# The last 256 tokens of a decoder layer's final product and norm, with tokens on partitions

## The chip, the cores and the metric

The kernel runs on one core of one Trainium2 chip. A core has five engines that work side by side and wait for each other by semaphores: TensorE (PE, matrix products into PSUM; its weight loads are shown as PEld), VectorE (DVE), ScalarE (ACT), GpSimd (POOL) and SyncE (SP), which issues the DMA transfers here. The metric is device time in microseconds for one execution; lower is better.

## The reference

One layer of a decoder: 1024 tokens, 1024 features, a windowed attention, an MLP with squared ReLU of hidden width 4096, and a final norm over the features of each token. The change lies in the last lines:

```python
def rms_norm(x, g):
    xf = x.astype(jnp.float32)
    y = xf * lax.rsqrt(jnp.mean(xf * xf, axis=-1, keepdims=True) + RMS_EPS)
    return (y * g.astype(jnp.float32)).astype(x.dtype)
...
def squared_relu_mlp(h, w_up, w_down):
    a = jax.nn.relu(h @ w_up)
    return (a * a) @ w_down
...
        h = h + mix
        h = h + squared_relu_mlp(rms_norm(h, mlp_norm[i]), mlp_w_up[i], mlp_w_down[i])
    return rms_norm(h, final_norm)
```

All data are float32.

## The kernel before

**Layout.** Features lie on the 128 partitions and tokens along the free dimension: the residual `h` is eight tiles `h[m]` of 128 features by 1024 tokens (`hr` in the profile). A norm therefore needs a sum over partitions, which TensorE makes with a column of ones (`colsum`, line 141; `n` in the profile), then the reciprocal root (`rstd`, line 146; `n_st`), then a diagonal matrix of it (`diag`, line 157; `dg`) and a product of ones with that diagonal which spreads one value per token over all partitions (`bcast`, line 161; `n3b`).

**Products.** Each float32 operand is split into a high part rounded to float32r and a low rest, and a product is three matmuls: high by high, high by low, low by high (lines 624 to 630). A matmul loads one operand of 128 by 128 into the array (LDWEIGHTS) and streams the other past it.

**The down projection.** It is made as seven products of half size (Strassen's scheme; lines 1082 to 1099 and `SEQ`), each of 16 groups of 128 hidden features. For every pair of groups, `operands` (line 1088) loads the hidden activations (`hr<-hid`) and one or two blocks of weights (`wd`, `we`), adds or subtracts these on VectorE (`wf`), and splits both operands on ScalarE (high, `dw_h`, `dx_h`) and VectorE (low, `dw_l`, `dx_l`). `evac` (line 1147) adds a finished product to `h`. The first six products run through lines 1162 to 1177 with 512 tokens per matmul.

**The last product** (lines 1179 to 1234) adds to the odd tiles `h[1], h[3], h[5], h[7]`, tokens 512 to 1023, alone; the even tiles are final before it. It keeps all its split operands in SBUF (`keep`) and runs in two halves. The first takes tokens 512 to 767, group by group as the operands come (`gg` counts pairs, 0 to 7; the prediction's "group" is such a pair, 24 matmuls). The second takes tokens 768 to 1023, four output blocks `mp` in turn, each over all 16 groups. In both a matmul loads 128 hidden features by 128 outputs of the weights and streams 256 tokens. Two generators, `fa` (tokens 0 to 511) and `fb` (512 to 767) of `finish` (line 1114), put the final norm of the earlier tokens between the matmuls, one step at each `next`. The norm of the last 256 tokens comes after all matmuls, with `h` times the gain (`hg`) prepared on ScalarE.

**What sets the order.** TensorE runs in the order of the program text (`pe.ordered`, line 167). From line 1065 on the compiler orders VectorE, ScalarE, GpSimd and SyncE itself: by its own estimate of when each is ready, so that a later instruction may stand ahead of an earlier one. Each engine then takes its queue strictly in that order. Temporary tiles come from rings: six of 128 by 1024 (`temp`, line 604: `wf`, `out`, `hg`), four of 128 by 512 (`sqtile`, line 607) and two PSUM tiles `mm` (`mmtile`, line 96).

Of the kernel before, what the change touches and what calls it, by code (L numbers as in the profile page):

```python
# [6 lines left out]
F32 = mybir.dt.float32  # L7
F32R = mybir.dt.float32r
I32 = mybir.dt.int32
AF = mybir.ActivationFunctionType  # L10
ALU = mybir.AluOpType
# [3 lines left out]
P = 128  # L15
T = 1024
DM = 1024
KT = DM // P
# [4 lines left out]
NG = DFF // (2 * P)  # L23
EPS = 1e-6
# [35 lines left out]
            self.steps.pop(0)()  # L60


def trunk(tc, xT, gains, wqkv, wo, wup, wdn, bias_d, sinks_d, ident_d, mask_d, outT):

# [7 lines left out]
    nc = tc.nc  # L74
    v, s, g, pe = (Ordered(tc, e) for e in (nc.vector, nc.scalar, nc.gpsimd, nc.tensor))

    const = tc.alloc_tile_pool(name="const", bufs=1)
# [3 lines left out]
    def atile(dt, name):  # L81
        return big.tile([P, 1024], dt, tag="A", name=name, bufs=16)
# [13 lines left out]
    def mmtile(name):  # L96
        return pmm.tile([P, 512], F32, tag="mm", name=name)

    ident = const.tile([P, P], F32, name="ident")
    ones = const.tile([P, P], F32, name="ones")  # L100
    mask = const.tile([P, P], I32, name="mask")
    gn = const.tile([P, 3, KT], F32, name="gn")
# [8 lines left out]
    def mm(out, lhsT, rhs, start, stop, **kw):  # L111
        pe.matmul(out, lhsT=lhsT, rhs=rhs, start=start, stop=stop, **kw)
        if tiny:
            tiny.pop(0)()

    def tr(out, in_):
        pe.transpose(out, in_, ident)
# [56 lines left out]
    def small(tag, name):  # L174
        return patt.tile([P, 512], F32, tag=tag, name=name)
# [7 lines left out]
    HALVES = (slice(0, 512), slice(512, 1024))  # L183
# [20 lines left out]
    for k in range(KT):  # L204
        xh = atile(F32R, f"xh{k}")
        xl = atile(F32R, f"xl{k}")
        for sl in HALVES if k < 2 else (slice(0, 1024),):
            nc.sync.dma_start(xr[k][:, sl], xT[:, k, sl])
            if k == 0 and sl.start == 0:
# [4 lines left out]
                                   op0=ALU.mult, op1=ALU.subtract)  # L214
# [32 lines left out]
    VV, KH, KL, h = [], [], [], []  # L247
# [240 lines left out]
    for hf in range(2):  # L488
        ps = small(("pv", "pt")[hf], f"n1_{hf}")
# [111 lines left out]
    def two(tile_):  # L601
        return tile_.rearrange("p (a c) -> p a c", a=2)

    def temp(name):
        return mlp.tile([P, 2, 512], F32, tag="t4", name=name, bufs=6)

    def sqtile(name):
        return mlp.tile([P, 512], F32, tag="sq", name=name, bufs=4)
# [47 lines left out]
    def stat_bcast(hf):  # L656
        ps = bank("Y", f"n2b{hf}")
        bcast(4, ps, stat.pop(("dg", hf)))
        return ps
# [230 lines left out]
    def oblock(m, hf):  # L890
        ps = bank(obanks[(hf * KT + m) % 5], f"o1_{m}_{hf}")
        for kk in range(4):
            mm3(ps, wsl(ws[m // 2], (m % 2) * 4 + kk), o_t[4 + kk], HALVES[hf], kk == 0, kk == 3)
        return ps
# [9 lines left out]
    rb = None  # L904
    for m in range(KT):
# [3 lines left out]
        ps = oblock(m, 1)  # L909
        if m == 0:  # L910
            stat_sum(0)
        if m == 1:
            rb = stat_bcast(0)
# [30 lines left out]
    rb = stat_bcast(1)  # L944
# [143 lines left out]
    def operands(n, gg, alloc):  # L1088
        a, b, op = DOWN[n]
        xr_ = two((qtile if n == SEQ[0] else ktile)(F32, f"hr{n}_{gg}"))  # L1090
        nc.sync.dma_start(xr_, hid[n - 1][gg])
        wr = two(rtile(f"wd{n}_{gg}"))
        nc.sync.dma_start(wr, wdn[a, gg])
        if op is not None:
            w2 = two(pptile(F32, f"we{n}_{gg}"))
            nc.sync.dma_start(w2, wdn[b, gg])
            wr_, wr = wr, temp(f"wf{n}_{gg}")
            v.tensor_tensor(wr, wr_, w2, op=op)
        return split2(wr, alloc, f"dw{n}_{gg}"), split2(xr_, alloc, f"dx{n}_{gg}")

    fin = {}

    def sumsq(key, parts, cols, eng):

        for m in parts:
            if key not in fin:
                fin[key] = sqtile(f"ssq3{key}")[:, 0:cols.stop - cols.start]
                s.activation(fin[key], h[m][:, cols], AF.Square)
            else:
                sq = sqtile(f"sq3_{key}_{m}")[:, 0:cols.stop - cols.start]  # L1110
                s.activation(sq, h[m][:, cols], AF.Square)
                eng.tensor_tensor(fin[key], fin[key], sq, op=ALU.add)

    def finish(t0, t1, sums, tags):

        sl, n = slice(t0, t1), t1 - t0
        nb = n // P
        ps_s = bank(tags[0], f"n3_{t0}")
        for i, sq in enumerate(sums):
            colsum(ps_s, sq, nb, i == 0, i == len(sums) - 1)  # L1120
        rn3 = rstd(ps_s, nb, f"n3_{t0}")
        dg = sqtile(f"dg{t0}")
        diag(rn3, 0, nb, dg)
        yield
        ps = bank(tags[1], f"n3b_{t0}")
        bcast(nb, ps, dg)
        if t1 == T:

            rb = ps[:, 0:n].unsqueeze(1)
            for i in range(2):  # L1130
                k, hg = 4 - i, hgs[i]
                v.tensor_tensor(hg[:, 0:k], hg[:, 0:k], rb.to_broadcast([P, k, n]), op=ALU.mult)
                if i:
                    v.scalar_tensor_tensor(hg[:, k], h[7][:, sl], gn[:, 2, 7:8], ps[:, 0:n],
                                           op0=ALU.mult, op1=ALU.mult)
                nc.sync.dma_start(outT[:, 4 * i:4 * i + 4, sl], hg)
            return
        for mp in range(4):
            yield
            out = temp(f"out{t0}_{mp}")  # L1140
            for e in range(2):
                m = 2 * mp + e
                v.scalar_tensor_tensor(out[:, e, 0:n], h[m][:, sl], gn[:, 2, m:m + 1], ps[:, 0:n],
                                       op0=ALU.mult, op1=ALU.mult)
            nc.sync.dma_start(outT[:, 2 * mp:2 * mp + 2, sl], out[:, :, 0:n])

    def evac(n, ps4, c0, c1):

        for mp, ps in enumerate(ps4):
            for mb, hf, sign in INTO[n]:  # L1150
                m = 2 * mp + mb
                dst = h[m][:, hf * 512 + c0:hf * 512 + c1]
                if sign > 0:
                    v.tensor_tensor(dst, ps, dst, op=ALU.add)
                else:
                    v.tensor_tensor(dst, dst, ps, op=ALU.subtract)
# [5 lines left out]
    for k, n in enumerate(SEQ[:-1]):  # L1162
# [8 lines left out]
        if k == 0:  # L1171
            h = []
# [6 lines left out]
    n = SEQ[-1]  # L1179
    keep = []  # L1180
    last_tags = [qtile] * 8 + [atile] * 8 + [wtile] * 6 + [otile] * 6 + [pptile, pptile, ktile, ktile]
    banks = [bank("X", f"d{n}_{i}") for i in range(3)] + [bank("Z", f"d{n}_3")]

    ps_q = [[banks[2 * q + mp % 2][:, (mp // 2) * 256:(mp // 2) * 256 + 256] for mp in range(4)] for q in range(2)]

    def lalloc(dt, name):
        return last_tags.pop(0)(dt, name)

    def mmq(q, g_, mp, first):
        (wh, wl), (xh, xl) = keep[g_]  # L1190
        c, tq = slice(mp * P, mp * P + P), slice(q * 256, q * 256 + 256)
        ps = ps_q[q][mp]
        mm(ps, wh[:, c], xh[:, tq], first, False, skip_group_check=True)
        mm(ps, wh[:, c], xl[:, tq], False, False, skip_group_check=True)
        mm(ps, wl[:, c], xh[:, tq], False, g_ == NG - 1, skip_group_check=True)

    fa = None
    hgs = []
    for gg in range(NG // 2):
        wv_, xv_ = operands(n, gg, lalloc)  # L1200
        for e in range(2):
            keep.append((wv_[e], xv_[e]))
            for mp in range(4):
                mmq(0, 2 * gg + e, mp, 2 * gg + e == 0 and mp < 2)
        if gg < 4:
            sumsq("b", (2 * gg,), HALVES[1], g)
        if gg == 4:
            fa = finish(0, 512, [fin["a"]], ("Y", "Y"))
        if gg >= 4 and gg % 2 == 0:
            next(fa)  # L1210
    evac(n, ps_q[0], 0, 256)
    sumsq("c", (1, 3, 5, 7), slice(512, 768), v)
    fb = finish(512, 768, [fin["b"][:, 0:256], fin["c"]], ("mm", "mm"))
    for mp in range(4):
        for g_ in range(NG):
            mmq(1, g_, mp, g_ == 0 and mp < 2)
            if g_ in (5, 11):
                next(fa, None)
            if mp > 0 and g_ in (3, 13):
                next(fb, None)  # L1220
        dst = h[2 * mp + 1][:, 768:1024]
        v.tensor_tensor(dst, ps_q[1][mp], dst, op=ALU.add)
        if mp < 3:
            sumsq("d", (2 * mp + 1,), slice(768, 1024), v)
            if mp % 2 == 0:
                hgs.append(temp(f"hg{mp}").rearrange("p a c -> p (a c)").rearrange("p (a c) -> p a c", a=4))
            for m in (2 * mp, 2 * mp + 1) if mp < 2 else (4, 5, 6):
                s.activation(hgs[m // 4][:, m % 4], h[m][:, 768:1024], AF.Copy, scale=gn[:, 2, m:m + 1])
        else:
            sq = sqtile("sq3_last")[:, 0:256]  # L1230
            s.activation(sq, dst, AF.Square)
    for f in (fa, fb, finish(768, 1024, [fin["b"][:, 256:512], fin["d"], sq], ("Y", "Y"))):
        for _ in f:
            pass

    pml.release()
    dram.release()
# [40 lines left out]
```

## Time and profile before

| | |
|---|---|
| time, median of 3 runs | 931.25 us (930.19 to 934.24) |
| profiled execution | 930.74 us |
| its span | 929.0 us |
| TensorE busy | 98% of the span |
| VectorE, ScalarE, GpSimd busy | 74%, 48%, 31% |
| last product's first matmul | 868.84 us |
| last VectorE instruction starts | 924.22 us |

The profile is one execution as recorded on the chip. A row of its timeline gives the start in us from the span's beginning, the duration in us, the engine, the line (here nearly always L41, a helper that records every operation), the operation, output<-inputs by the program's names, and the shape; in brackets stands how long the engine was idle before, and what it waited for. A row "x4" merges four instructions. A row of the groups gives the count, the total us and the mean ns of one. Matmuls overlap: the distance between two starts tells their pace, not their duration. A row of the stretches (from:to) lists for each engine the busy us and instructions, then TensorE's granted clock, the busy share of the DMA engines and their GB/s.

### The profile page before, as it was taken

What the parts mean: (1) busy time and instruction counts of PE and PEld (TensorE: products, weight loads), DVE (VectorE), ACT (ScalarE), POOL (GpSimd) and SP (SyncE); (2) the same over time, 40 slices, a digit from 0 to 9 for tenths busy, and PEclk for the clock granted to TensorE, in tenths of its full rate; (3) what the DMA queues carried; (4) which work ended last, traced back from release to release, by engine and by line L of the source; (5) the groups of instructions that cost most, each with busy time, mean ns of one, the idle gap of its engine ahead of it and who ended that gap; (6) DMA issues with size and microseconds to landing.
All of it is one profiled execution on the core that took longest, in us unless ns stands there. A gap on an engine that the chain in (4) does not pass through costs nothing.

```text
span 929.0 us, 12593 instructions
## 1 busy us (share of the span) xinstructions
PE 910.4 (98%) x4508; PEld 766.4 (82%) x4508; DVE 689.6 (74%) x952; ACT 446.9 (48%) x855; POOL 289.7 (31%) x255
## 2 busy tenths in 40 slices
PE   8999999999999999999999999999999999999996
PEld 7788888888878787888888888788888888888995
DVE  7789988999838998866666575556878786568953
ACT  8578878777524374333333433343343333445511
POOL 1026656566265025664454434110000000040200
PEclk9999999999999999999999999999999999999998
DMA  8200100501354016644444454799788998448522
GB/s 312 69 29 29 53 23 13 204 29 47 115 174 165 1 62 232 205 159 155 164 157 137 145 170 172 274 335 408 286 311 298 339 338 314 164 158 272 205 92 90
DMA packets 57438, 160.36 MB, mean 173 GB/s; under 512 B 6432, under 2 KB 10272, under 8 KB 57376
## 3 DMA queue, kind: packets, MB, share of 16 engines
q1 hardware_dynamic: 57376, 159.57, 48.7%
q8 instruction: 35, 0.57, 0.3%
q14 instruction: 27, 0.22, 0.1%
HBM read 121.79 MB, written 37.75 MB: 172 GB/s over the span
## 4 chain that ended last, share of the span: by engine, by line
PE 86%; DVE 7%; ACT 3%; DMA 1%; issue 1%; POOL 1%; SPq 0%; DVEq 0%; ACTq 0%
PE d L41 33%; PE uX L41 16%; PE f L41 12%; PE uY L41 9%; PE uZ L41 4%; PE pv L41 3%; PE S L41 3%; PE o L41 2%; PE pt L41 1%; PE psv L41 1%; PE psk L41 1%; DMA wu0b<-wup 1%; DVE h L41 1%; DVE oa L41 1%; DVE ta L41 1%
## 5 line engine op out<-in xcount | busy, mean ns | idle before, releaser
L41 PE MATMUL d<-dx_h,dw_h 128*128 128x512 f32 (+1 forms) x512 | 186.3, 364 | 0.0
L41 PE MATMUL d<-dx_h,dw_l 128*128 128x512 f32 (+1 forms) x512 | 185.6, 362 | 0.0
L41 PE MATMUL d<-dx_l,dw_h 128*128 128x512 f32 (+1 forms) x512 | 185.6, 362 | 0.0
L41 PEld LDWEIGHTS d<-dx_l,dw_h 128*128 128x128 f32 x512 | 96.6, 189 | 15.2 <-issue 0.2
L41 PEld LDWEIGHTS d<-dx_h,dw_h 128*128 128x128 f32 x512 | 96.6, 189 | 15.2 <-issue 0.2
L41 PEld LDWEIGHTS d<-dx_h,dw_l 128*128 128x128 f32 x512 | 96.6, 189 | 15.1
L41 ACT CAST dw_h<-wf 128x1024 fp32r<-128x1024 f32 x40 | 41.9, 1051 | 100.0 <-PE d L41 79.4
L41 DVE TENSOR_TENSOR dx_l<-hr,dx_h 128x1024 fp32r<-128x1024 f32 x56 | 71.7, 1287 | 13.6 <-ACT dx_h L41 13.6
L41 POOL TENSOR_TENSOR ssq3a<-ssq3a,sq_a 128x512 f32<-128x512 f32 x7 | 11.7, 1665 | 212.0 <-ACT sq_a L41 211.6
L41 ACT CAST dx_h<-hr 128x1024 fp32r<-128x1024 f32 x56 | 58.5, 1049 | 36.5 <-DMA hr<-hid 35.1
L41 DVE TENSOR_TENSOR dw_l<-wf,dw_h 128x1024 fp32r<-128x1024 f32 x40 | 49.6, 1242 | 25.5 <-ACT dw_h L41 25.3
L41 POOL TENSOR_TENSOR t<-t,sm 128x512 f32<-128x512 f32 x32 | 33.3, 1041 | 109.9 <-DVE sm L41 109.9
L41 DVE TENSOR_TENSOR wf<-wd,we 128x1024 f32<-128x1024 f32 x40 | 49.4, 1248 | 19.6 <-DMA we<-wdn 12.4
L41 ACT ACTIVATE t<-t,sm 128x129 f32<-128x129 f32 x128 | 50.5, 396 | 11.1 <-DVE sm L41 10.6
L41 PE MATMUL f<-xh,w_h 128*128 128x512 f32 x128 | 53.3, 416 | 0.0
L41 PE MATMUL f<-xl,w_h 128*128 128x512 f32 x128 | 50.4, 394 | 0.0
L41 PE MATMUL f<-xh,w_l 128*128 128x512 f32 x128 | 50.2, 393 | 0.0
L41 POOL TENSOR_TENSOR ob<-ob,oa 128x512 f32<-128x512 f32 x16 | 23.3, 1454 | 78.8 <-DVE ob L41 75.3
L41 ACT COPY oa<-uX 128x512 f32<-128x512 f32 x32 | 18.8, 586 | 55.7 <-PE uX L41 55.7
L41 PE MATMUL uX<-xu_h,wb 128*128 128x512 f32 x128 | 42.1, 390 | 0.7 <-ACT oa L41 0.7
L41 POOL TENSOR_TENSOR oc<-oc,oa 128x512 f32<-128x512 f32 x16 | 21.7, 1358 | 62.3 <-DVE oc L41 62.3
L41 POOL TENSOR_SCALAR_AFFINE_SELECT cur<-hl 128x1024 fp32r<-128x1024 f32 x32 | 39.4, 1233 | 2.0 <-DVE hl L41 2.0
(367 smaller groups left out, 2399.4 us busy)
## 6 DMA issues: line engine op xcount, KB each, us to landing
wd<-wdn SPq DMA_DIRECT2D x56, 512.0 KB, 5.5
hr<-hid SPq DMA_DIRECT2D x56, 512.0 KB, 4.9
we<-wdn SPq DMA_DIRECT2D x40, 512.0 KB, 7.2
hid<-oa SPq DMA_DIRECT2D x32, 256.0 KB, 2.6
hid<-oc SPq DMA_DIRECT2D x32, 256.0 KB, 2.5
hid<-ob SPq DMA_DIRECT2D x32, 256.0 KB, 2.5
w_r<-wqkv SPq DMA_DIRECT2D x8, 512.0 KB, 4.1
h<-xT SPq DMA_DIRECT2D x8, 512.0 KB, 6.3
```

Source lines behind the costliest of these rows:

```text
L41: ins = method(*args, **kw)
```

## The change

The last 256 tokens become two tails of 128 tokens. In a tail the roles in the matmul are swapped: the activations of 128 tokens are loaded and 512 outputs of the weights are streamed, so that the result lies with tokens on partitions and all 512 features of the odd blocks along the free dimension. What of `h` belongs to these tokens is turned by transposes on TensorE, in four calls of `turn` behind pairs 4 to 7 of the first half: the even blocks are squared and summed (ScalarE) and multiplied by the gain row `grow` (VectorE), the odd blocks copied. `grow`, the gain of all features on every partition (512 KB), is a new input, loaded behind the operands of pair 2. `last` adds the product, sums squares along the free dimension, takes the reciprocal root per partition, scales and stores both halves into a new output `outB`, which the host puts behind the other 768 tokens. The squares of the even blocks (`sumsq("b", ...)`) cover tokens 512 to 767 only, where they covered 512 to 1023; the branch of `finish` for the last tokens, its column sums, diagonal and broadcast are gone. The steps of `fa` and `fb` stand at other groups.

```diff
-    ps_q = [[banks[2 * q + mp % 2][:, (mp // 2) * 256:(mp // 2) * 256 + 256] for mp in range(4)] for q in range(2)]
+    ps_q = [banks[mp % 2][:, (mp // 2) * 256:(mp // 2) * 256 + 256] for mp in range(4)]
...
+    tails = [768, 896]
+    hT, sE, grow = {}, {}, []
+
+    def turn(t0, e):
+
+        if t0 not in hT:
+            hT[t0] = temp(f"hT{t0}")
+            sE[t0] = const.tile([P, 4], F32, name=f"sE{t0}")
+        ps = mmtile(f"tr{t0}_{e}")
+        for mp in range(4):
+            tr(ps[:, mp * P:mp * P + P], h[2 * mp + e][:, t0:t0 + P])
+        if e:
+            s.copy(hT[t0][:, 1], ps)
+        else:
+            sq = sqtile(f"sqT{t0}")
+            s.activation(sq, ps, AF.Square, accum_out=sE[t0][:, 0:1])
+            v.tensor_tensor(hT[t0][:, 0], ps, grow[0][:, 0], op=ALU.mult)
+            v.tensor_scalar(sE[t0][:, 1:2], sE[t0][:, 0:1], 1.0 / DM, EPS, op0=ALU.mult, op1=ALU.add)
+
+    def last(i, t0, ps):
+
+        x, st = hT[t0], sE[t0]
+        tt = const.tile([P, 4], F32, name=f"tt{t0}")
+        var, y0, b_, y = (tt[:, k:k + 1] for k in range(4))
+        v.tensor_tensor(x[:, 1], ps, x[:, 1], op=ALU.add)
+        sq = sqtile(f"sqL{t0}")
+        s.activation(sq, x[:, 1], AF.Square, accum_out=st[:, 2:3])
+        v.tensor_tensor(x[:, 1], x[:, 1], grow[0][:, 1], op=ALU.mult)
+        s.activation(y, st[:, 2:3], AF.Sqrt, bias=st[:, 1:2], scale=1.0 / DM)
+        v.tensor_scalar(var, st[:, 2:3], 1.0 / DM, st[:, 1:2], op0=ALU.mult, op1=ALU.add)
+        v.reciprocal(y0, y)
+        v.tensor_tensor(b_, y0, y0, op=ALU.mult)
+        v.scalar_tensor_tensor(b_, b_, -0.5, var, op0=ALU.mult, op1=ALU.mult)
+        v.scalar_tensor_tensor(st[:, 3:4], b_, 1.5, y0, op0=ALU.add, op1=ALU.mult)
+        s.activation(x[:, 0], x[:, 0], AF.Copy, scale=st[:, 3:4])
+        v.tensor_scalar(x[:, 1], x[:, 1], st[:, 3:4], None, op0=ALU.mult)
+        nc.sync.dma_start(outB[i, :, 1], x[:, 1])
+        nc.sync.dma_start(outB[i, :, 0], x[:, 0])
+
     fa = None
     for gg in range(NG // 2):
         wv_, xv_ = operands(n, gg, lalloc)
+        if gg == 2:
+            grow.append(temp("grow"))
+            nc.sync.dma_start(grow[0], grow_d)
...
         if gg < 4:
-            sumsq("b", (2 * gg,), HALVES[1], g)
+            sumsq("b", (2 * gg,), slice(512, 768), g)
+        else:
+            turn(tails[gg // 2 - 2], gg % 2)
         if gg == 4:
             fa = finish(0, 512, [fin["a"]], ("Y", "Y"))
         if gg >= 4 and gg % 2 == 0:
             next(fa)
-    evac(n, ps_q[0], 0, 256)
+    evac(n, ps_q, 0, 256)
     sumsq("c", (1, 3, 5, 7), slice(512, 768), v)
-    fb = finish(512, 768, [fin["b"][:, 0:256], fin["c"]], ("mm", "mm"))
-    for mp in range(4):
+    fb = finish(512, 768, [fin["b"], fin["c"]], ("mm", "mm"))
+    for i, t0 in enumerate(tails):
+        ps = banks[2 + i]
         for g_ in range(NG):
-            mmq(1, g_, mp, g_ == 0 and mp < 2)
-            if g_ in (5, 11):
+            (wh, wl), (xh, xl) = keep[g_]
+            tq = slice(t0 - 512, t0 - 512 + P)
+            mm(ps, xh[:, tq], wh, g_ == 0, False, skip_group_check=True)
+            mm(ps, xh[:, tq], wl, False, False, skip_group_check=True)
+            mm(ps, xl[:, tq], wh, False, g_ == NG - 1, skip_group_check=True)
+            if g_ in (2, 5, 8, 11):
                 next(fa, None)
-            if mp > 0 and g_ in (3, 13):
+            if i == 0 and g_ in (9, 14) or i and g_ in (0, 3, 6):
                 next(fb, None)
...
-    for f in (fa, fb, finish(768, 1024, [fin["b"][:, 256:512], fin["d"], sq], ("Y", "Y"))):
-        for _ in f:
-            pass
+        if i:
+            for f in (fa, fb):
+                for _ in f:
+                    pass
+        last(i, t0, ps)
```

More of the change, by code (lines that the diff above doesn't have):

```diff
@@ L60, in run, with trunk @@
             self.steps.pop(0)()
-def trunk(tc, xT, gains, wqkv, wo, wup, wdn, bias_d, sinks_d, ident_d, mask_d, outT):
+def trunk(tc, xT, gains, wqkv, wo, wup, wdn, bias_d, sinks_d, ident_d, mask_d, grow_d, outT, outB):
     nc = tc.nc
@@ L1126, in finish @@
         bcast(nb, ps, dg)
[L1127 to L1137, printed above, removed]
         for mp in range(4):
@@ L1182, in trunk, with mmq @@
     banks = [bank("X", f"d{n}_{i}") for i in range(3)] + [bank("Z", f"d{n}_3")]
-    ps_q = [[banks[2 * q + mp % 2][:, (mp // 2) * 256:(mp // 2) * 256 + 256] for mp in range(4)] for q in range(2)]
+    ps_q = [banks[mp % 2][:, (mp // 2) * 256:(mp // 2) * 256 + 256] for mp in range(4)]
     def lalloc(dt, name):
         return last_tags.pop(0)(dt, name)
-    def mmq(q, g_, mp, first):
+    def mmq(g_, mp, first):
         (wh, wl), (xh, xl) = keep[g_]
-        c, tq = slice(mp * P, mp * P + P), slice(q * 256, q * 256 + 256)
-        ps = ps_q[q][mp]
+        c, tq = slice(mp * P, mp * P + P), slice(0, 256)
+        ps = ps_q[mp]
         mm(ps, wh[:, c], xh[:, tq], first, False, skip_group_check=True)
@@ L1195, in mmq @@
         mm(ps, wl[:, c], xh[:, tq], False, g_ == NG - 1, skip_group_check=True)
+    tails = [768, 896]
[32 more added lines that the diff above has]
+        nc.sync.dma_start(outB[i, :, 0], x[:, 0])
     fa = None
-    hgs = []
     for gg in range(NG // 2):
         wv_, xv_ = operands(n, gg, lalloc)
+        if gg == 2:
+            grow.append(temp("grow"))
+            nc.sync.dma_start(grow[0], grow_d)
         for e in range(2):
@@ L1203, in trunk @@
             for mp in range(4):
-                mmq(0, 2 * gg + e, mp, 2 * gg + e == 0 and mp < 2)
+                mmq(2 * gg + e, mp, 2 * gg + e == 0 and mp < 2)
         if gg < 4:
-            sumsq("b", (2 * gg,), HALVES[1], g)
+            sumsq("b", (2 * gg,), slice(512, 768), g)
+        else:
+            turn(tails[gg // 2 - 2], gg % 2)
         if gg == 4:
@@ L1210, in trunk @@
             next(fa)
-    evac(n, ps_q[0], 0, 256)
+    evac(n, ps_q, 0, 256)
     sumsq("c", (1, 3, 5, 7), slice(512, 768), v)
-    fb = finish(512, 768, [fin["b"][:, 0:256], fin["c"]], ("mm", "mm"))
-    for mp in range(4):
+    fb = finish(512, 768, [fin["b"], fin["c"]], ("mm", "mm"))
+    for i, t0 in enumerate(tails):
+        ps = banks[2 + i]
         for g_ in range(NG):
-            mmq(1, g_, mp, g_ == 0 and mp < 2)
-            if g_ in (5, 11):
+            (wh, wl), (xh, xl) = keep[g_]
[4 more added lines that the diff above has]
+            if g_ in (2, 5, 8, 11):
                 next(fa, None)
-            if mp > 0 and g_ in (3, 13):
+            if i == 0 and g_ in (9, 14) or i and g_ in (0, 3, 6):
                 next(fb, None)
[L1221 to L1231, printed above, removed]
-    for f in (fa, fb, finish(768, 1024, [fin["b"][:, 256:512], fin["d"], sq], ("Y", "Y"))):
-        for _ in f:
-            pass
+        if i:
[3 more added lines that the diff above has]
+        last(i, t0, ps)
     pml.release()
@@ L1265 @@
     arrays["bias"] = bias.reshape(KT, 2, P, P).transpose(0, 2, 1, 3)
+    arrays["grow"] = np.broadcast_to(a["final_norm"].reshape(4, 2, P).transpose(1, 0, 2).reshape(1, 2, 512), (P, 2, 512))
     arrays["ident"] = np.eye(P, dtype=np.float32)
@@ L1271 @@
     d = {n: nc.dram_tensor(n, x.shape, mybir.dt.from_np(x.dtype), kind="ExternalInput").ap() for n, x in arrays.items()}
-    out = nc.dram_tensor("outT", (P, KT, T), F32, kind="ExternalOutput").ap()
+    out = nc.dram_tensor("outT", (P, KT, 768), F32, kind="ExternalOutput").ap()
+    out_b = nc.dram_tensor("outB", (2, P, 2, 512), F32, kind="ExternalOutput").ap()
     with tile.TileContext(nc) as tc:
         trunk(tc, d["xT"], d["gains"], d["wqkv"], d["wo"], d["wup"], d["wdn"], d["bias"], d["sinks"],
-              d["ident"], d["mask"], out)
+              d["ident"], d["mask"], d["grow"], out, out_b)
     r = _run(nc, [arrays], core_ids=[0])
-    return np.ascontiguousarray(r.results[0]["outT"].transpose(2, 1, 0).reshape(1, T, DM))
+    first = r.results[0]["outT"].transpose(2, 1, 0).reshape(768, DM)
+    rest = r.results[0]["outB"].reshape(2, P, 2, 4, P).transpose(0, 1, 3, 2, 4).reshape(256, DM)
+    return np.ascontiguousarray(np.concatenate([first, rest]).reshape(1, T, DM))
```

## The prediction

> **What bounds the kernel now.** I read first the page's busy times, then the last stage engine by engine in the timeline.
>
> ```profile
> span 929.0 us, 12593 instructions
> PE 910.4 (98%) x4508; PEld 766.4 (82%) x4508; DVE 689.6 (74%) x952; ACT 446.9 (48%) x855; POOL 289.7 (31%) x255
> ```
>
> TensorE is busy nearly all the span, so time can go in two ways only: fewer microseconds of TensorE's own queue, or a shorter tail in which TensorE has finished and the rest of the chip works on the last outputs. The tail is read from three extracts of the timeline: the last rows of TensorE, of VectorE and of ScalarE.
>
> ```profile
> 917.84 0.28 PE L41 MATMUL d<-dx_h,dw_l 128*128 128x256 f32 x1
> 917.96 0.50 PE L41 MATMUL n<-ones,ssq3b 128*128 128x1 f32 x4
> 918.32 0.58 PE L41 MATMUL n<-ones,ssq3d 128*128 128x1 f32 x4
> 919.14 0.61 PE L41 MATMUL n<-ones,sq_last 128*128 128x1 f32 x4 [0.24 <-ACT sq_last L41]
> 921.42 0.76 PE L41 MATMUL n3b<-dg,ones 128*128 128x256 f32 x2 [1.67 <-DVE dg L41]
> ```
>
> ```profile
> 918.16 0.42 DVE L41 TENSOR_TENSOR hr<-d,hr 128x256 f32<-128x256 f32 x1 [4.37 <-PE d L41]
> 920.08 0.16 DVE L41 TENSOR_SCALAR n_st<-n 128x2 f32<-128x2 f32 x1 [1.50 <-ACT n_st L41]
> ...
> 920.94 0.42 DVE L41 TENSOR_TENSOR dg<-ident,n_st 128x256 f32<-128x256 f32 x1
> 922.22 2.09 DVE L41 TENSOR_TENSOR hg<-hg,n3b 128x1024 f32<-128x1024 f32 x2 [0.85 <-PE n3b L41]
> 924.22 0.48 DVE L41 SCALAR_TENSOR_TENSOR hg<-hr,gn,n3b 128x256 f32<-128x256 f32 x1
> ```
>
> ```profile
> 918.68 0.42 ACT L41 ACTIVATE sq_last<-hr 128x256 f32<-128x256 f32 x1 [4.94 <-DVE hr L41]
> 919.79 0.26 ACT L41 ACTIVATE n_st<-n,eps 128x2 f32<-128x2 f32 x1 [0.70 <-PE n L41]
> ```
>
> The last product matmul ends at 917.84 + 0.28 = 918.12, and the span ends at 929.0: a tail of 10.88 us in which nothing is hidden. It is a chain from engine to engine: residual add, square, column sums, the reciprocal root, the diagonal, the broadcast, the scaling, the stores. VectorE ends at 924.22 + 0.48 = 924.70; the last 4.30 us are the store and the closing of the program.
>
> **The second half of the last product.** Before, it is 192 matmuls of 256 token columns; after, 96 of 512 output columns, with the activations as the loaded operand. Both shapes stand side by side where the product before last ends and the last begins:
>
> ```profile
> 863.63 0.39 PE L41 MATMUL d<-dx_l,dw_h 128*128 128x512 f32 x1
> ...
> 868.62 0.39 PE L41 MATMUL d<-dx_h,dw_l 128*128 128x512 f32 x1
> 868.84 0.28 PE L41 MATMUL d<-dx_h,dw_h 128*128 128x256 f32 x1
> ...
> 883.12 0.28 PE L41 MATMUL d<-dx_h,dw_l 128*128 128x256 f32 x1
> ```
>
> The wide ones start every (868.62 - 863.63) / 22 = 0.2268 us, the narrow ones every (883.12 - 868.84) / 119 = 0.1200 us. From the first start to the last end the half took 191 x 0.1200 + 0.28 = 23.20 us and will take 95 x 0.2268 + 0.39 = 21.94: **-1.26 us**. Its bounds are 0 (the swapped operand costs what the wide shape wins) and -1.3. The column sums and the broadcast of tokens 512 to 767 stay between the matmuls in both. The Trainium skill (TensorE: Matmul & The Clock Gate, Back-to-back issue gap) gives N / 2.4 + 2.5 ns for an isolated matmul, 109 and 216 ns here, so that halving the count would win only 0.2 us; this trace has 120 and 227 ns, and by the page's figures the sum below would be -2.1 us.
>
> **The transposes.** Four groups of four go into TensorE's queue behind groups 4 to 7 of the first half. The attention stage has the same operation between the same wide matmuls:
>
> ```profile
> 152.57 0.60 PE L41 MATMUL pt<-ident,t 128*128 128x128 f32 x4
> 152.93 0.48 PE L41 MATMUL f<-xh,w_h 128*128 128x512 f32 x1
> 153.24 0.39 PE L41 MATMUL f<-xl,w_h 128*128 128x512 f32 x1
> ```
>
> A group takes 0.36 us from its start to the next matmul, and that matmul is longer than the one behind it. From the group to the second matmul are 0.67 us, where one spacing would be 0.23: 0.44 us a group, 1.76 for four. The groups behind 4 and 6 stand directly before the column sums and the broadcast of tokens 0 to 511, whose return to the product is paid anyway, so I take **+1.7 us**; the bounds are 4 x 0.36 = 1.4 and 4 x 0.60 = 2.4.
>
> ```profile
> L41 PE MATMUL pt<-ident,t x128: 270/272/331, 60.0 to 238.0; 128*128 128x128 f32 x128
> ```
>
> This is the transpose alone, 0.272 us of duration; paid one after another sixteen would be 4.4 us, which the group of four in 0.36 us speaks against. The Trainium skill (the same page, Part 4: PE-mode transpose) gives about 275 ns for one; counted singly that is 4.4 us and a sum of -0.5 us, and the duration agrees here but the spacing does not.
>
> The groups also need a free PSUM tile, and their readers on VectorE and ScalarE must have run before the group two places on may start. These readers, and VectorE's multiplication by the gain row, are queued among the operand splits:
>
> ```profile
> 876.96 3.44 DVE L41 TENSOR_TENSOR wf<-wd,we 128x1024 f32<-128x1024 f32 x2
> 880.33 1.21 DVE L41 TENSOR_TENSOR dx_l<-hr,dx_h 128x1024 fp32r<-128x1024 f32 x1
> 881.47 1.21 DVE L41 TENSOR_TENSOR dw_l<-wf,dw_h 128x1024 fp32r<-128x1024 f32 x1
> 882.60 1.21 DVE L41 TENSOR_TENSOR dx_l<-hr,dx_h 128x1024 fp32r<-128x1024 f32 x1
> 883.74 1.21 DVE L41 TENSOR_TENSOR dw_l<-wf,dw_h 128x1024 fp32r<-128x1024 f32 x1
> 884.87 0.15 DVE L41 TENSOR_SCALAR n_st<-n 128x4 f32<-128x4 f32 x1
> ```
>
> By lines and places the last four splits are those of groups 6 and 7, and they end at 883.74 + 1.21 = 884.95. TensorE wants group 7 at 868.84 + 168 x 0.12 = 889.0 at the earliest: 4 us of cover. Against it stand VectorE's new multiplication (0.68 us, by a row below) with a tiny instruction, and the load of the gain row, 512 KB, which SyncE issues behind the loads of group 2 and ahead of those of groups 3 to 7:
>
> ```profile
> 860.00:870.00 10.00, 10.00 (x50) 8.47 (x49) 8.77 (x8) 4.96 (x5) 0.00 (x0) 1.00 1.02 383
> ```
>
> The DMA engines are full there at 383 GB/s, so those loads come 512 KB / 383 = 1.4 us later. 1.4 + 0.8 = 2.2 of 4 us: I cost the load and VectorE's work at nothing. Without that cover TensorE would pay the excess, up to 2.2 us. GpSimd's squares of the even blocks halve their width, which nobody waits for. The first 128 tokens' norm runs beside the 48 matmuls (10.9 us) of the second 128.
>
> **The tail.** What is left behind the last matmul, with the nearest row for each step:
>
> ```profile
> L41 DVE TENSOR_TENSOR hr<-d,hr 128x512 f32<-128x512 f32 x36 | 22.6, 681 | 0.0
> ```
>
> ```profile
> L41 ACT ACTIVATE sq_a<-hr 128x512 f32<-128x512 f32 x7 | 4.2, 626 | 3.3 <-DVE hr L41 2.3 <-POOL ssq3a L41 1.0
> ```
>
> ```profile
> 100.05 0.19 ACT L41 ACTIVATION_READ_ACCUMULATOR t<-t,sm 128x1 f32 x1
> 100.14 0.57 ACT L41 COPY t<-S 128x512 f32<-128x512 f32 x1
> ```
>
> ```profile
> L41 DVE TENSOR_TENSOR x<-ta,x 128x512 f32<-128x512 f32 x4 | 2.7, 684 | 0.0
> ```
>
> ```profile
> L41 ACT ACTIVATE xh<-xr,gn 128x512 fp32r<-128x512 f32 x4 | 2.8, 715 | 2.7 <-DMA gn<-gains 1.6 <-DMA xr<-xT 1.1
> ```
>
> Counted from the last matmul's end: the residual add starts at 0.04 (918.16 - 918.12) and ends at 0.72. The square starts 0.10 later, as 918.68 did behind 918.58, takes 0.63, and its row sum is read out by one more instruction (0.19, of which some 0.1 comes on top): 1.55. VectorE meanwhile multiplies by the gain row, which may start when the square has read its input, 0.68 us until about 2.15; the square root (0.26) lies under that. From the variance to the finished root were 920.94 - 920.08 = 0.86 us before, and it is the same five instructions: 2.96. ScalarE then scales the even blocks (0.07 to start, 0.715) until 3.75, while VectorE scales the odd ones in at most 0.68. Column sums (0.61), diagonal (0.42), broadcast (0.76) and the scaling of 2.09 + 0.48 us are gone. For the stores:
>
> ```profile
> DMA to landing us min/median/max: 3.0/3.1/3.2
> ```
>
> ```profile
> outT<-out SPq DMA_DIRECT2D x4, 256.0 KB, 2.1
> ```
>
> The first line is that of the two 512 KB stores that end the kernel, the second that of the 256 KB stores of tokens 512 to 767. Of the 4.30 us behind VectorE's end 3.1 were landing and 1.20 issue and closing. Now the last store is one of two of 256 KB, less than half a microsecond apart: 2.3 us, nearer the second row. The tail is 3.75 + 1.20 + 2.3 = 7.25 instead of 10.88: **-3.6 us**. Bounds: with 2.1 of landing and the gain multiplication behind the root's steps in VectorE's order, 6.8; with 3.1 of landing and the two stores' issue in each other's way (0.4), 8.4. So -4.1 to -2.4.
>
> **The sum** is -1.26 + 1.7 - 3.6 = -3.2 us, between -4.0 (all low ends) and 0 (all high ends). The profiled execution took 930.74 us, 0.5 below the median of the runs, 931.25 (930.19 to 934.24). It becomes 927.5, the median **928.0 us**.
>
> **The rivals.** *Slower: the gain multiplications stand too early in VectorE's queue.* VectorE takes its instructions in the order that the compiler gave them. If the multiplication behind group 4's transposes stands ahead of the row at 876.96, VectorE waits for TensorE's group 4 (883.24 with 0.4 of transposes), and the 5.6 us from that row to 882.60 come after 884.5: group 6 is ready at 890.1, where TensorE wants it at about 887.9 (883.24, a group of 2.88, two groups of transposes and the column sums): 2.2 us. The same ahead of group 7's two splits costs 2.3 more. That is +1.3 us in all, **932.5 us**; it decides from 3.2 us of stall on. Against it speaks the row at 884.87: an instruction of VectorE written at that place, and waiting for the column sums behind group 4, stands behind the last split. For it: the order may change with the program. *The stores set the end:* both 256 KB transfers land as late as the 512 KB ones and the tail is 8.4 us: -2.0 us, **929.2**. For it: they run together. *The transposes run one by one:* 4.4 us instead of 1.7, -0.5 us, **930.7**; the change then does almost nothing. The group rows speak against it. *A faster case:* the tail falls under 6 us, for which no row speaks, or every low end holds and the runs scatter down: 926.5.
>
> **How the numbers follow.** The forecast has 0.70, the store-bound tail 0.12, the late splits 0.08, the single transposes 0.04, the faster case 0.06. 0.5% (4.7 us) is about what a measurement of this kernel can tell from no change; the lines are 926.6 and 935.9. The forecast and all rivals but the last lie between them; with the scatter of the runs at the lower line I give faster 0.12, and slower 0.04 for stalls beyond the one priced: same 0.84. The range runs from 926.0 (the low ends and 1 us of scatter) to 931.3 (the high ends), which leaves out most of the late splits.
>
> **What would show it.** Right: wide rows every 0.227 us in the second half, four groups of transposes of 0.4 us, no idle time on TensorE in the first half, about 3.0 us from the last matmul to the root, stores landing in 2.1 to 2.5. Wrong: TensorE waiting for a split or for the reader of a transposed tile, a tail above 8.4 us, or narrow and wide halves of equal length.

## The result, and the profile after

The changed kernel takes 940.07 us (median of 4 runs, 939.54 to 941.81); the kernel before, on the same chip, 930.72 us. The ratio is 1.0102 [1.0086, 1.0118]: slower by 9.4 us, where 928.0 with a range of 926.0 to 931.3 was forecast. The forecast is wrong, in sign too.

The head of the page, span and busy times:

```profile
span 938.7 us, 12416 instructions
PE 914.8 (97%) x4414; PEld 766.1 (82%) x4414; DVE 688.1 (73%) x957; ACT 447.6 (48%) x857; POOL 290.6 (31%) x255
```

The busy share of TensorE barely moves (98 to 97%) and the span is 9.7 us longer. TensorE runs 94 matmuls fewer and is busy for 4.4 us more. So a part of the loss is waiting, and another part is matmuls that take longer. The waits of TensorE (us in total, times, longest) have two lines that the list of the kernel before does not have:

```profile
PE d L41 <- ACT dw_h L41: 6.1, 2, 3.2
PE d L41 <- DVE dw_l L41: 1.1, 2, 0.6
```

Twice TensorE stands still in the last product until the split weights come, 7.2 us in all. Its timeline shows where, and what follows:

```profile
882.46 0.28 PE L41 MATMUL d<-dx_h,dw_l 128*128 128x256 f32 x1
882.58 0.60 PE L41 MATMUL tr<-ident,hr 128*128 128x128 f32 x4
883.02 0.95 PE L41 MATMUL n<-ones,ssq3a 128*128 128x1 f32 x8
887.14 0.57 PE L41 MATMUL d<-dx_h,dw_h 128*128 128x256 f32 x1 [3.18 <-ACT dw_h L41]
887.51 0.41 PE L41 MATMUL d<-dx_l,dw_h 128*128 128x256 f32 x1
888.48 0.58 PE L41 MATMUL d<-dx_h,dw_l 128*128 128x256 f32 x1 [0.55 <-DVE dw_l L41]
888.86 0.41 PE L41 MATMUL d<-dx_h,dw_h 128*128 128x256 f32 x1
...
893.13 0.41 PE L41 MATMUL d<-dx_h,dw_l 128*128 128x256 f32 x1
...
901.35 0.58 PE L41 MATMUL d<-dx_h,dw_h 128*128 128x256 f32 x1 [2.91 <-ACT dw_h L41]
```

The first stall is at pair 5, directly behind the transposes and column sums of pair 4; the second, at 901.35, at pair 7, behind the transposes and broadcast of pair 6. After each, the narrow matmuls start every (893.13 - 888.86) / 20 = 0.213 us instead of 0.12. The stretches of 5 us give the clock that goes with it (busy us and count of PE, PEld, DVE, ACT, POOL; granted clock; DMA share; GB/s):

```profile
885.00:890.00 5.00, 2.31 (x9) 2.01 (x10) 5.00 (x8) 3.04 (x3) 0.00 (x0) 0.72 0.00 2
890.00:895.00 5.00, 5.00 (x29) 5.00 (x29) 1.37 (x2) 0.59 (x1) 0.00 (x0) 0.60 0.02 3
895.00:900.00 5.00, 3.44 (x24) 2.61 (x23) 1.66 (x3) 0.69 (x2) 0.00 (x0) 1.00 0.00 0
900.00:905.00 5.00, 3.07 (x12) 2.78 (x13) 5.00 (x8) 1.04 (x1) 0.00 (x0) 0.58 0.29 109
```

Each row is a mean over 5 us. In slices of 0.5 us the granted clock is 0.50 for some 6.8 us at each stall, from 887.2 to 894.0 and from 900.8 to 907.7, and 1.00 before and after. Those slow matmuls count as busy, which is why the busy share hides them.

Why do the weights come late? VectorE's timeline between the same times:

```profile
872.32 1.21 DVE L41 TENSOR_TENSOR dx_l<-hr,dx_h 128x1024 fp32r<-128x1024 f32 x1
884.00 0.69 DVE L41 TENSOR_TENSOR hT<-tr,grow 128x512 f32<-128x512 f32 x1 [10.46 <-ACT sqT L41]
...
884.82 1.19 DVE L41 TENSOR_TENSOR wf<-wd,we 128x1024 f32<-128x1024 f32 x1
...
886.00 1.22 DVE L41 TENSOR_TENSOR wf<-wd,we 128x1024 f32<-128x1024 f32 x1
...
887.21 1.22 DVE L41 TENSOR_TENSOR dw_l<-wf,dw_h 128x1024 fp32r<-128x1024 f32 x1
...
898.34 0.69 DVE L41 TENSOR_TENSOR hT<-tr,grow 128x512 f32<-128x512 f32 x1 [6.97 <-ACT sqT L41]
...
899.01 1.21 DVE L41 TENSOR_TENSOR wf<-wd,we 128x1024 f32<-128x1024 f32 x1
```

VectorE idles for 10.46 us ahead of the gain multiplication of the first tail (`hT<-tr,grow`), which waits for transposes that TensorE reaches only at 882.58. Behind it stand the weight sums `wf` of pairs 5 and 6, and behind the second tail's multiplication that of pair 7. Their operands have been in SBUF for long: from 875 to 885 the DMA engines move nothing. SyncE issues the stage's last load at

```profile
866.23 0.42 SPq L1096 DMA_DIRECT2D we<-wdn  x1
```

In the kernel before, the sum for pair 5 ran well ahead of the matmuls that need it, the last two followed at 876.96, and no split was late:

```profile
869.04 1.22 DVE L41 TENSOR_TENSOR wf<-wd,we 128x1024 f32<-128x1024 f32 x1
```

(ScalarE's high part `dw_h` needs `wf`, so TensorE's wait is put down to ScalarE; it is VectorE's order that is late.)

### The profile page after: what moved, and what is told of

Same layout as the page of the kernel before. It is cut to its first block, busy times and chain, and to the rows that moved or that the text cites. A ratio compares the mean times of both kernels' runs of the same rounds, so it can differ in the third digit from the quotient of the medians.

```text
span 938.7 us, 12416 instructions
## 1 busy us (share of the span) xinstructions
PE 914.8 (97%) x4414; PEld 766.1 (82%) x4414; DVE 688.1 (73%) x957; ACT 447.6 (48%) x857; POOL 290.6 (31%) x255
## 4 chain that ended last, share of the span: by engine, by line
PE 85%; DVE 7%; ACT 3%; issue 1%; DMA 1%; POOL 1%; SPq 0%; DVEq 0%; ACTq 0%
PE d L41 33%; PE uX L41 16%; PE f L41 12%; PE uY L41 8%; PE uZ L41 4%; PE pv L41 3%; PE S L41 3%; PE o L41 2%; PE pt L41 1%; PE psv L41 1%; PE psk L41 1%; DVE h L41 1%; DMA wv_r<-wqkv 1%; DMA wu0b<-wup 1%; DVE oa L41 1%
## 5 line engine op out<-in xcount | busy, mean ns | idle before, releaser
L41 PE MATMUL d<-dx_h,dw_h 128*128 128x512 f32 (+1 forms) x448 | 170.0, 379 | 6.1 <-ACT dw_h L41 6.1
L41 PE MATMUL d<-dx_h,dw_l 128*128 128x512 f32 (+1 forms) x448 | 169.9, 379 | 1.1 <-DVE dw_l L41 1.1
L41 PE MATMUL d<-dx_l,dw_h 128*128 128x512 f32 (+1 forms) x448 | 169.6, 379 | 0.0
L41 PEld LDWEIGHTS d<-dx_h,dw_h 128*128 128x128 f32 x448 | 86.5, 193 | 21.8 <-ACT dw_h L41 7.0
L41 PEld LDWEIGHTS d<-dx_h,dw_l 128*128 128x128 f32 x448 | 86.5, 193 | 16.8 <-DVE dw_l L41 1.7
L41 PEld LDWEIGHTS d<-dx_l,dw_h 128*128 128x128 f32 x448 | 86.6, 193 | 15.1
L41 ACT ACTIVATE t<-t,sm 128x129 f32<-128x129 f32 x128 | 50.5, 397 | 10.9 <-DVE sm L41 10.4
```

What stands on the lines that cost most here:

```text
L41: ins = method(*args, **kw)
```

## The experiments

**Theories.** All explain a gain multiplication ahead of the weight sums, or deny that it matters.
- *Ring:* temporaries of one ring (`temp`, six tiles) are handed out in the order of the program text. `hT768` is first written behind pair 4's transposes and stands in the text ahead of the sums of pairs 5 and 6, `hT896` ahead of that of pair 7. A sum cannot be placed ahead of the first write of an earlier tile of its ring.
- *Queue:* the compiler puts a VectorE instruction that waits for TensorE there, whatever tile it writes.
- *Shortage:* `hT768`, `hT896` and `grow` hold three of six tiles, so that a sum waits for a free one.
- For the slow matmuls: *clock*, a granted clock that falls while TensorE is idle; against it *piecemeal*, operands that trickle in.

Each ratio is to the kernel before on the same chip: 930.39 us for claim_both_early, claim_first_early and the two probes, 929.85 for keep_clock, turn_late, claim_both_again and claim_and_fuse, 930.04 for keep_clock_short and changed_again.

**claim_both_early**: the changed kernel, with both `hT` tiles claimed and first written, by a tiny memset on GpSimd, at pair 2. All else stays.

```diff
+    def claim(t0):
+        hT[t0] = temp(f"hT{t0}")
+        sE[t0] = const.tile([P, 4], F32, name=f"sE{t0}")
+        g.memset(hT[t0][:, 0, 0:1], 0.0)
...
             nc.sync.dma_start(grow[0], grow_d)
+            for t0 in tails:
+                claim(t0)
```

> The changed kernel, with one addition: behind the load of the gain row (pair 2) both hT tiles are taken from the ring of temporaries and one column of each is set to zero by GpSimd, so that they have their place before the weight sums wf of pairs 3 to 7 ask for theirs. Nothing else moves. Ring theory (temporaries are handed out in the order of the text, so wf of pairs 5 and 6 wait for hT768, which waits for TensorE's transposes, and wf of pair 7 for hT896): no stall of TensorE above 0.5 us in the first half, no half clock, and the 3.2 us of the forecast, 927.5 us against 930.7 before (926.5 to 928.5). Queue theory (the gain multiplication goes first on VectorE because it stands ahead in the text, whatever tile it writes): unchanged, 940. Shortage theory (three of six temporaries are held to the end, and three are too few for the weight sums): unchanged or worse, 940 or more.

Measured: 926.39 us (926.17 to 927.92), ratio 0.9954 [0.9942, 0.9967], as the ring theory has it and 0.1 us below its range. Its VectorE:

```profile
872.85 2.89 DVE L41 TENSOR_TENSOR wf<-wd,we 128x1024 f32<-128x1024 f32 x2
...
879.07 1.21 DVE L41 TENSOR_TENSOR dw_l<-wf,dw_h 128x1024 fp32r<-128x1024 f32 x1
883.30 0.69 DVE L41 TENSOR_TENSOR hT<-tr,grow 128x512 f32<-128x512 f32 x1 [3.02 <-ACT sqT L41]
```

All sums and splits are done by 880.28, ahead of the multiplication, and TensorE's waits no longer name `d`. The multiplication still waits for TensorE, harmlessly. The tiles are held longer than in the changed kernel, so *shortage* falls; the multiplications themselves are unchanged, which speaks against *queue*.

**claim_first_early**: the same for the first tail alone.

```diff
+            for t0 in tails[:1]:
+                claim(t0)
```

> As the run with both tiles taken early, but only hT768; hT896 is taken by its own first writer as in the changed kernel. The changed kernel loses about 12.5 us against the forecast (9.3 measured and 3.2 not won). Ring theory: the first of the two stalls goes, the second stays, about half of the loss comes back: 934 us (932.5 to 935.5), with one idle stretch of TensorE at pair 7. Queue theory: 940. Shortage theory: 940.

Measured: 934.38 us (933.25 to 935.34), ratio 1.0037 [1.0024, 1.0049]: between the two. The stall at pair 5 is gone, that at pair 7 stays, with its slow matmuls; from its waits, its chain and its stretches:

```profile
PE d L41 <- ACT dw_h L41: 2.9, 1, 2.9
```

```profile
895.03 5.06 PE d L41 x22
```

```profile
895.00:900.00 5.00, 4.97 (x23) 4.97 (x24) 3.03 (x5) 0.00 (x0) 0.00 (x0) 0.50 0.79 297
```

Each tile holds back the sums that follow it in the text, and no others.

**probe_in_ring** and **probe_own_tile**: the kernel *before*, with two tiny instructions behind pairs 4 and 6: one matmul of ones, and a copy of one column of its result to a tile that nobody reads. The tile comes from the ring in the first and stands alone in the second.

```diff
+            ps = mmtile(f"probe_ps{gg}")
+            mm(ps[:, 0:P], ones, ones, True, True)
+            pr = temp(f"probe{gg}")            # in probe_in_ring
+            pr = const.tile([P, 2, 2], F32, name=f"probe{gg}")   # in probe_own_tile
+            v.tensor_copy(pr[:, 0, 0:1], ps[:, 0:1])
             next(fa)
```

> The kernel before, with two small additions: behind the matmuls of pairs 4 and 6 of the first half one matmul of ones into a PSUM tile, and a VectorE copy of one column of it into a temporary of the same ring as wf. Nothing reads the copy. No transposes, no gain row, no new tail. Ring theory: two stalls as in the changed kernel, at pairs 5 and 7, some 12 us with the slower clock: 943 us (940 to 945). Queue theory: the same 943. Shortage theory (the temporaries are given back at once): 931.

> The kernel before with the same two matmuls and two VectorE copies, but the copies go into small tiles of their own and not into the ring. Ring theory: no stall, 931.3 us (the matmuls cost some 0.3 each). Queue theory: 943, as with the ring's tiles. Shortage theory: 931.

Measured: 940.09 us (938.57 to 941.34), ratio 1.0098 [1.0082, 1.0113], with the tile in the ring; 930.89 (929.85 to 932.97), 1.0004 [0.9994, 1.0013], with a tile of its own. VectorE with the ring's tile, and then with its own:

```profile
882.29 0.16 DVE L41 COPY probe<-probe_ps 128x1 f32<-128x1 f32 x1 [8.10 <-PE probe_ps L41]
882.37 1.23 DVE L41 TENSOR_TENSOR wf<-wd,we 128x1024 f32<-128x1024 f32 x1
```

```profile
875.54 3.44 DVE L41 TENSOR_TENSOR wf<-wd,we 128x1024 f32<-128x1024 f32 x2
882.31 1.21 DVE L41 TENSOR_TENSOR dw_l<-wf,dw_h 128x1024 fp32r<-128x1024 f32 x1
884.27 0.16 DVE L41 COPY probe<-probe_ps 128x1 f32<-128x1 f32 x1 [0.75 <-PE probe_ps L41]
```

Two copies of 0.16 us cost the old kernel 9.7 us when they claim a tile of the ring, and nothing measurable when they do not. Where the tile comes from decides whether the sums run ahead; *queue* falls. A claim in the ring brings about such a loss with no transposes, no gain row and no wide matmuls in the kernel. The 940.09 us are less than the 943 expected, and 9.7 us less than the 13.4 worked out for the changed kernel below, since TensorE's waits are shorter, 5.2 us in all instead of 7.2:

```profile
PE d L41 <- ACT dw_h L41: 3.3, 2, 1.7
PE d L41 <- DVE dw_l L41: 1.9, 2, 1.1
```

The clock falls here too, to 0.50 in slices of 0.5 us, for some 3.4 us each time instead of 6.8, though no single wait is above 1.7 us. (The compiler's rule itself is not shown, only the order that it gives; and no run separates asking for a tile from first writing it, as both were moved together.)

**keep_clock**: the changed kernel, with 28 matmuls of ones into a bank that the first half does not use, behind each `next(fa)` at pairs 4 and 6, to fill the stalls.

```diff
+            for _ in range(NWARM):
+                mm(banks[2][:, 0:P], ones, ones, True, True)
```

> The changed kernel with 28 matmuls of ones (128x128, some 0.11 us each) behind the column sums of pair 4 and behind the broadcast of pair 6, where TensorE stands idle for 3 to 5 us. Their result is overwritten. Clock theory (behind each stall 22 matmuls take 5.06 us instead of 2.64 because the granted clock fell while TensorE was idle): the idle time is filled, the clock stays, and 2 x 2.4 = 4.8 us come back: 935.5 us against 940.1 (934 to 937), with the narrow matmuls at 0.12 us behind the stalls. Piecemeal theory (they are slow because their operands come one by one): 940.

Measured: 938.92 us (938.7 to 940.59), ratio 1.0097 [1.0083, 1.0111]; the expected time is missed. Its TensorE shows why:

```profile
882.40 0.95 PE L42 MATMUL n<-ones,ssq3a 128*128 128x1 f32 x8
883.22 6.50 PE L42 MATMUL d<-ones 128*128 128x128 f32 x56
889.47 0.36 PE L42 MATMUL d<-dx_h,dw_h 128*128 128x256 f32 x1
```

The fill was too long: it runs for 889.47 - 883.22 = 6.25 us, where the stall that it was to fill lasted 3.18. A matmul of ones stands in the profile as two records of 0.11 us (x56 for 28), and I had priced it as one. Counted from the column sums, the product resumes 889.47 - 882.40 = 7.07 us later, where the changed kernel takes 4.12 (887.14 - 883.02). The granted clock stays at 1.00 from 880 to 910, but what this won was lost in length, so the run decides nothing by its time.

**keep_clock_short**: the same with 18 matmuls.

> As the run with 28 matmuls of ones behind pairs 4 and 6, with 18 of them. 28 took 6.25 us each time (two passes of 0.11 us a matmul) and ended 2.3 us behind the moment at which the changed kernel's first operand was ready; 18 take 4.0 us and end before the stall does. Clock theory: granted clock 1.00 throughout, the narrow matmuls at 0.12 us, the stalls themselves untouched: 4.8 us less than the changed kernel on the same chip (4 to 5.5), 935.3 us. Piecemeal theory: no less.

Measured: 935.81 us (935.12 to 937.88), ratio 1.0059 [1.0042, 1.0076]. The stretches and two rows of the chain:

```profile
885.00:890.00 5.00, 5.00 (x48) 5.00 (x46) 3.93 (x9) 2.67 (x5) 0.00 (x0) 1.00 0.02 5
890.00:895.00 5.00, 4.85 (x41) 4.64 (x40) 3.45 (x5) 1.91 (x3) 0.00 (x0) 1.00 0.00 0
```

```profile
890.55 2.90 PE d L42 x22
...
902.35 2.90 PE d L42 x22
```

The clock stays at 1.00 and the 22 matmuls behind each stall take 2.90 us where the changed kernel's take 5.06. The splits come as late as before: the first matmul that needs a low part starts 890.55 - 885.09 = 5.46 us behind the start of the column sums, as in the changed kernel (888.48 - 883.02 = 5.46). Beside **changed_again**, the changed kernel on the same chip

> The changed kernel once more, on the same chip as the run with 18 matmuls of ones: 1.010 of before (1.0086 to 1.0118).

which took 940.94 us (939.68 to 941.73), ratio 1.0115 [1.01, 1.013], filling the stalls wins 5.1 us: *clock* holds, *piecemeal* falls.

**turn_late**: the changed kernel, with the four calls of `turn` moved behind the loop over the pairs, so that every sum stands in the text ahead of `hT`.

```diff
-        else:
-            turn(tails[gg // 2 - 2], gg % 2)
...
+    for t0 in tails:
+        for e in range(2):
+            turn(t0, e)
     evac(n, ps_q, 0, 256)
```

> The changed kernel with the four calls of turn moved behind the last pair of the first half, ahead of the residual add of tokens 512 to 767. hT768 and hT896 then ask for their temporaries after all weight sums, without being taken early. Ring theory: as with both tiles taken early, 926.5 (925.5 to 928), with perhaps 1 us lost where the third call waits for a PSUM tile. Queue theory: the multiplications now stand behind all splits in the text, the same. It separates nothing between these two; it tells whether early claiming is needed, or only another place in the text.

Measured: 928.02 us (927.32 to 928.29), ratio 0.9976 [0.9966, 0.9986]. The late splits are gone in this way too, so another place in the text is enough; between *ring* and *queue* this decides nothing, since both have it so. The time lies at the upper end of the range expected (925.5 to 928). The four groups now stand together, and the second pair waits for the readers of the first (a wait of its list):

```profile
PE tr L41 <- ACT hT L41: 0.9, 1, 0.9
```

**claim_both_again** is claim_both_early once more.

> The run with both hT tiles taken early once more, on the same chip as the next one: 0.9954 of before, as measured (0.994 to 0.997).

Measured: 927.05 us (926.39 to 930.14), ratio 0.9965 [0.9952, 0.9979], beside turn_late's 928.02. On both chips it beats the kernel before.

**claim_and_fuse**: claim_both_early, with the gain multiplication and the scaling of the odd blocks as one instruction behind the root, and their store issued by ScalarE instead of SyncE.

```diff
-        v.tensor_tensor(x[:, 1], x[:, 1], grow[0][:, 1], op=ALU.mult)
...
-        v.tensor_scalar(x[:, 1], x[:, 1], st[:, 3:4], None, op0=ALU.mult)
-        nc.sync.dma_start(outB[i, :, 1], x[:, 1])
+        v.scalar_tensor_tensor(x[:, 1], x[:, 1], st[:, 3:4], grow[0][:, 1], op0=ALU.mult, op1=ALU.mult)
+        nc.scalar.dma_start(outB[i, :, 1], x[:, 1])
```

> Both hT tiles taken early; in last the multiplication of the odd blocks by the gain row and the scaling by the root become one instruction of VectorE behind the root, and the odd blocks are stored from ScalarE's queue, so that the two stores don't wait for each other's issue. By the tail of the run with both taken early: the root's steps start 0.6 us sooner, the last store is issued 0.4 us sooner behind the scaling: 0.7 to 1.0 us less, 925.5 (0.9945 of before). If the stores' landing sets the end and not their issue, 0.6.

Measured: 926.23 us (925.93 to 927.77), ratio 0.9961 [0.9948, 0.9973]. The median is 0.8 us below claim_both_again's, the size expected, but the intervals overlap and the 925.5 us expected is missed, so no gain is shown. In the tail, where it was to come from, the profiles show next to none. The last store is issued 3.39 us behind the last matmul's end instead of 3.95, but the two stores now start at one time and land later; first claim_both_early's landing, then this kernel's:

```profile
DMA to landing us min/median/max: 2.0/2.3/2.5
```

```profile
DMA to landing us min/median/max: 2.5/2.7/2.8
```

So the 0.56 us are given back to the transfers; from the last matmul to the span's end it is 7.15 us instead of 7.19 in claim_both_early.

## Why the prediction was wrong

I compare from the last product's first matmul (868.84 before, 868.18 after, 867.49 in claim_both_early) to the span's end, since the stretch ahead of it varies by a few us from one execution to the next. That stage takes 60.16 us before, 70.52 after and 57.11 in claim_both_early. Without the late splits the change brings -3.05 us, where -3.2 was forecast; with them it costs 13.4 us more.

**The terms that held.** claim_both_early shows them undisturbed, in the chain:

```profile
882.05 0.44 PE tr L41 x4
882.49 0.79 PE n L41 x8
...
886.25 0.44 PE tr L41 x4
...
889.57 0.44 PE tr L41 x4
890.00 0.86 PE n3b L41 x2
...
893.73 0.44 PE tr L41 x4
894.16 6.83 PE d L41 x30
...
901.78 3.58 PE d L41 x15
...
905.78 11.62 PE d L41 x51
917.41 0.02 issue
```

- *Second half:* 6.83 + 3.58 + 11.62 = 22.03 us of wide matmuls (forecast 21.94). The kernel before has, in its chain, 10.07, 3.70 and 12.24 us for 216 narrow ones, of which 24 belong to pair 7: 26.01 - 24 x 0.12 = 23.13. That is -1.10 for the forecast -1.26. The swapped operand costs nothing.
- *Transposes:* four groups of 0.44 us are 1.76, forecast 1.7. Counted singly by their duration they would have been 4.4; the pace of a group decides.
- *Tail:* 924.6 - 917.41 = 7.19 us, forecast 7.25; 10.88 before. So -3.7 for -3.6.

**The step that failed** is "I cost the load and VectorE's work at nothing", and behind it the price and the chance of the rival that had the gain multiplications too early in VectorE's queue. The load was free. The order was not, for three reasons.

First, the evidence. Against that rival I set one row: "an instruction of VectorE written at that place, and waiting for the column sums behind group 4, stands behind the last split." But that row writes `n_st`, which is not of the ring of `wf`, and `hT` is. probe_own_tile and probe_in_ring are those two cases side by side, 930.89 and 940.09. An instruction's place was read off one that claimed something else. That the new tile comes from `temp` stood in the diff, and that `wf` does too in the kernel's description.

Second, what is held back. I let the multiplication delay the splits of groups 6 and 7 only, by 2.2 and 2.3 us. It held back the sums, and the first of them, for pair 5, stood at 869.04 before, ahead of the row at 876.96 from which I counted; TensorE wants that pair right behind pair 4. So nothing hides the chain from the transposes to the operands: transposes, square, multiplication, sum, high part, low part. Against claim_both_early TensorE's first matmul behind the inserts comes 3.3 and 3.1 us later (887.14 - 883.02 = 4.12 where its chain has 0.79; 901.35 - 897.42 = 3.93 where it has 0.86), and the wait for the low part costs 1.1 us more each time (888.48 - 887.14 = 1.34 where two spacings are 0.24): 8.6 us.

Third, the clock, which I had not in the sum at all. The 22 matmuls behind each stall take 5.06 us instead of 22 x 0.12 = 2.64: 4.8 us for both. At clock 1.00, in keep_clock_short, they take 2.90, so 2 x (5.06 - 2.90) = 4.3 us of this are the clock's own and the rest stays at full clock; the time fell there by 5.1, in medians whose runs scatter by some 2 us. The Trainium skill (TensorE: Matmul & The Clock Gate, Part 1: The HAM clock gate) has the clock at half after an idle window of about 3.4 us; the trace agrees in the half and has it earlier. The clock falls some 3.2 us after the first wait begins and some 2.4 after the second, and in probe_in_ring waits of 1.69 and 1.07 us with two matmuls between them were enough. A single wait of 1.62 us in the attention stage of the kernel before leaves it at 1.00. The runs do not show where between these the limit lies.

8.6 + 4.8 = 13.4 us, as the stages differ; -3.05 + 13.4 = +10.4 for the stage. The stretch ahead of it was 0.7 us shorter in the changed kernel's profile, so the spans differ by 9.7, and the medians by 9.4. "It decides from 3.2 us of stall on" was right, and so was the rival's direction; it had 8 chances in 100 and a third of its price.

The signs that the forecast gave named the fault ("TensorE waiting for a split") and the parts that held (pace 0.227, groups of 0.4, stores in 2.1 to 2.5).

## What to carry to other kernels

Look where each new tile comes from. As the compiler ordered this kernel, the first write to a tile of a shared ring also fixes the place of all later tiles of that ring, so a tile whose first writer waits for a slow engine needs a claim early in the text, a ring of its own, or a place behind the tiles that others wait for.

When the place of an instruction in a queue is inferred from another instruction, that one must write to the same pool of tiles. And a wait of TensorE of some 3 us, or two close together of 1.7 and 1.1, is to be priced well above its length, since the matmuls behind it run at half the clock: 7.2 us of waits in the list cost 13.4 here.

The version to keep is the change with both tiles claimed early: 0.9954 [0.9942, 0.9967] and 0.9965 [0.9952, 0.9979] of the kernel before, 4.0 and 2.8 us, about what was forecast.

## What was not expected of the hardware

- A fill of TensorE with 18 matmuls of ones, whose result nobody uses, made the changed kernel 5.1 us faster.
- The granted clock fell to 0.50 and stayed there for some 6.8 us at the changed kernel's stalls and some 3.4 us at the shorter ones of probe_in_ring, at the first of which the matmuls had run on at full pace for 1.2 us before it fell.
- Two stores of 256 KB issued at the same time by SyncE and ScalarE landed in 2.5 to 2.8 us, and 0.4 us apart by SyncE alone in 2.0 to 2.5, so that the tail won only 0.04 us.
